# Hybrid decoder trunk: another order of the three products in the two-chunk steps of its linear attention

## The chip, the cores and the metric

The kernel runs on one core of a Trainium2 chip. The metric is the device time of one execution in microseconds (us), as the median of several runs. The core has five engines with a queue each: TensorE (PE, matrix products; its weight loads are listed apart as PEld), VectorE (DVE), ScalarE (ACT), GpSimd (POOL) and SyncE (SP, which issues DMAs). They meet through semaphores. PE writes into PSUM, which is divided into banks of 512 float32 columns on 128 partitions; DVE and ACT read the results from there.

## What is computed

The reference is one layer of a decoder trunk on 2048 tokens (and 16 meta tokens ahead of them) with 1024 channels. One input projection feeds two branches, a Mamba-2 scan (SSD) and gated linear attention (GLA); each goes through a gate and a projection, and an output projection with the residual and a final norm ends it. The change lies in the GLA branch:

```python
def gla_chunked(q, k, v, log_a, chunk, state0):
    ...
    def step(s, inp):
        qi, ki, vi, gi = inp
        o_inter = jnp.einsum('bhtk,bhkv->bhtv', qi * jnp.exp(gi), s)
        ...
        att = jnp.einsum('bhtk,bhsk,bhtsk->bhts', qi, ki, rel)
        o_intra = jnp.einsum('bhts,bhsv->bhtv', att, vi)
        g_last = gi[:, :, -1]
        k_dec = ki * jnp.exp(g_last[:, :, None, :] - gi)
        s_new = jnp.exp(g_last)[..., None] * s + jnp.einsum('bhsk,bhsv->bhkv', k_dec, vi)
        return s_new, o_inter + o_intra
```

There are 4 heads of 128 key and 256 value channels. Per chunk and head there are three products: the **state product** (queries times the state `s`), the **attention product** (attention matrix times values), and the **key product** (decayed keys times values). The first two are added and are the chunk's output. The third goes into the **state update**, which makes the state for the next chunk.

## The kernel before, in words

The tokens are cut into 4 blocks of 512 (`BLK`), each into 4 chunks of 128 (`NCH`). In the first part (up to about 1530 us) every block goes through 4 SSD groups and 4 GLA heads: `ssd_proj` and `gla_proj` are generators that do the projections on PE, and between their pieces `step()` advances the scans that are running beside them (`ssd_scan`, `gla_scan`, the gates, the loading of the next block). So a scan is a generator too, and what stands between two of its `yield`s goes into PE's queue in one piece, between two pieces of projection. The second part (gate, branch and output projections) isn't touched.

PE's and SP's queues hold their instructions in the order in which the code is written (`manual_schedule`). The framework orders those of DVE, ACT and POOL itself, by a model of the engines, and places the semaphores by what the tiles need.

`accum(ps, stat, mov, first, last)` (lines 189 to 191) is a product in three matmuls: both operands are split into a high and a low float32r part, and high x high, high x low and low x high are added in `ps`. The values (`got["v"]`), the decayed keys (`kdt`) and the attention matrix (`atp`) exist as such pairs; in the profile the values are named `tok`. The state product (line 846) is one float32 matmul, which appears twice in the trace (x2 per chunk).

The last stage of `gla_scan` goes through the chunks in a loop, lines 841 to 853, two chunks in each step, since it yields after every odd chunk. Per chunk there is one PSUM bank `po` from the pool `pc` (of two banks): columns 256 to 511 take the key product, columns 0 to 255 the sum of attention product and state product. PE does, for every chunk, the key product (line 844), the attention product (845) and the state product (846). DVE then does the state update (847), in place in `s_gla`, reading the key product in the bank. ACT copies the output half of the bank to `ot` (849) and sums its squares (851), after the update. The odd chunk's state product reads what the even chunk's update wrote. 4 blocks x 4 heads x 2 make 32 such steps with 64 chunks.

[...]

Of the kernel before, what the change touches and what calls it, by code (L numbers as in the profile page):

```python
# [14 lines left out]
P = 128  # L15
# [25 lines left out]
def trunk_kernel(ctx: ExitStack, tc: tile.TileContext, xm, xmt, w_feat, w_tok, w_zm, w_br, w_o,  # L41
                 cf32, cmsk, pvec, fnw, hvec, gw2, out):
    nc = tc.nc
# [5 lines left out]
    def mk(pool, shape, dt, tag, **kw):  # L49
        cnt[0] += 1  # L50
        return pool.tile(shape, dt, tag=tag, name=f"{tag}_{cnt[0]}", **kw)
# [83 lines left out]
    def bank(pool, tag):  # L135
        return mk(pool, [P, 512], F32, tag)
# [20 lines left out]
    s_gla = const.tile([P, GH, 256], F32, name="s_gla")  # L157
# [29 lines left out]
    def accum(ps, stat, mov, first, last, **kw):  # L187
        (sh, sl), (mh, ml) = stat, mov
        nc.tensor.matmul(ps, sh, mh, start=first, stop=False, **kw)  # L189
        nc.tensor.matmul(ps, sh, ml, start=False, stop=False, **kw)  # L190
        nc.tensor.matmul(ps, sl, mh, start=False, stop=last, **kw)  # L191
# [480 lines left out]
    def gla_proj(o, h):  # L672
        got = {"gs": []}
        keys = yield from gla_keys(o, h)
        last = o.b == nblk - 1
        if last and h == GH - 1:
            begin(gla_scan(o, h, *keys, got))
            yield
            got["v"] = yield from gla_values(o, h)
            yield  # L680
            yield from gla_gates(o, h - 1, held_gates.pop())
            yield from gla_gates(o, h, got["gs"])
        else:
            yield
            got["v"] = yield from gla_values(o, h)
            if last and h == GH - 2:
                begin(gla_scan(o, h, *keys, got))
                held_gates.append(got["gs"])
                yield
            else:  # L690
                yield
                yield from gla_gates(o, h, got["gs"])
                begin(gla_scan(o, h, *keys, got))
# [3 lines left out]
    def gla_scan(o, h, qs, kf, got):  # L697
# [19 lines left out]
        qg = mk(wk, [P, META + BLK], F32, "act", bufs=NACT)[:, :BLK]  # L717
# [57 lines left out]
        kdt = [mk(wk, [P, NCH, P], F32R, "kdt", bufs=2) for _ in range(2)]  # L775
# [54 lines left out]
        atp = [mk(wk, [P, NCH, P], F32R, "atp", bufs=2) for _ in range(2)]  # L830
# [10 lines left out]
        for c in range(NCH):  # L841
            po = bank(pc, "pc")
            vc = [t[:, c] for t in got["v"][0]]
            accum(po[:, 256:], [t[:, c] for t in kdt], vc, True, True)
            accum(po[:, :256], [t[:, c] for t in atp], vc, True, False)
            nc.tensor.matmul(po[:, :256], qg[:, c * P:(c + 1) * P], s_gla[:, h], start=False, stop=True)
            nc.vector.scalar_tensor_tensor(s_gla[:, h], s_gla[:, h], egl[:, c:c + 1], po[:, 256:],
                                           op0=ALU.mult, op1=ALU.add)
            nc.scalar.activation(ot[:, c], po[:, :256], AF.Copy)
            jk = mk(wk, [P, 256], BF16, "junk", bufs=1)  # L850
            nc.scalar.activation(jk, po[:, :256], AF.Square, accum_out=ssq[:, c:c + 1])
            if c % 2:
                yield
# [372 lines left out]
```

## Time and profile before

| | |
|---|---|
| median of 3 runs | 2328.28 us (2320.05 to 2328.89) |
| the profiled execution | 2335.47 us |
| its span, first to last instruction | 2333.7 us |
| mean granted clock of PE | 0.988 |
| PE busy | 2243.4 us |
| state products (L846) in the trace | 128 pieces, median 379 ns |
| state updates (L847) | 64, median 479 ns |

The profile is of one execution, by the hardware profiler. A row of its timeline has the start, the length, the engine, the line, the operation, what is written and read (by the program's names without numbers: `pc` is a bank of that pool) and the shapes; in brackets stands the idle time of the engine just before, and what ended it. Matmuls are pipelined, so one starts before the one ahead of it has ended, and their ends are modelled. A list of waits has per row who waited, for whom, how long in total and how often. In a list of the program's order `[waits DVE_49]` says that the instruction waits for a semaphore that DVE raises. No time is in such a list.

### The profile page before, as it was taken

What the parts mean: (1) busy time and instruction counts of PE and PEld (TensorE: products, weight loads), DVE (VectorE), ACT (ScalarE), POOL (GpSimd) and SP (SyncE); (2) the same over time, 40 slices, a digit from 0 to 9 for tenths busy, and PEclk for the clock granted to TensorE, in tenths of its full rate; (3) what the DMA queues carried; (4) which work ended last, traced back from release to release, by engine and by line L of the source; (5) the groups of instructions that cost most, each with busy time, mean ns of one, the idle gap of its engine ahead of it and who ended that gap; (6) DMA issues with size and microseconds to landing.
All of it is one profiled execution on the core that took longest, in us unless ns stands there. A gap on an engine that the chain in (4) does not pass through costs nothing.

```text
span 2333.7 us, 36472 instructions
## 1 busy us (share of the span) xinstructions
PE 2243.4 (96%) x12651; PEld 1956.5 (84%) x12651; DVE 1563.6 (67%) x2884; ACT 1188.9 (51%) x2764; POOL 687.6 (29%) x677
## 2 busy tenths in 40 slices
PE   6899999999999999999999999989999999999998
PEld 6889989888888988888988898868788888787886
DVE  5676766676675667566568655664679855788966
ACT  5665655465544455543456443464554454554443
POOL 3344433122321212221122200026424264423341
PEclk9999999999999999999999999999999999999999
DMA  7655865667786666777676655466668866778753
GB/s 254 225 203 200 293 234 195 210 206 222 264 271 190 207 221 211 253 244 234 187 236 214 216 168 164 140 222 207 221 227 275 283 224 215 260 247 276 226 189 108
DMA packets 300937, 515.89 MB, mean 221 GB/s; under 512 B 27616, under 2 KB 143584, under 8 KB 300752
## 3 DMA queue, kind: packets, MB, share of 16 engines
q1 hardware_dynamic: 221840, 422.15, 55.7%
q10 hardware_dynamic: 78912, 91.41, 11.3%
q8 instruction: 99, 1.62, 0.3%
q14 instruction: 86, 0.70, 0.1%
HBM read 366.26 MB, written 147.19 MB: 220 GB/s over the span
## 4 chain that ended last, share of the span: by engine, by line
PE 48%; DMA 9%; DVE 7%; issue 4%; ACT 3%; SPq 1%; POOL 1%; ACTq 0%; DVEq 0%; POOLq 0%
PE pj L189 7%; PE pj L191 7%; PE pj L190 7%; PE psa L189 4%; PE psa L191 4%; PE psa L190 4%; DMA br<-br_t 2%; PE psb L191 2%; PE psb L190 2%; PE psb L189 2%; PE pc L756 1%; DMA br<-gate_t 1%; DVE b L960 1%; DVE a L984 1%; DMA acc<-in_xmt 1%
## 5 line engine op out<-in xcount | busy, mean ns | idle before, releaser
L189 PE MATMUL pj<-u,whl 128*128 128x512 f32 (+1 forms) x1184 | 448.7, 379 | 13.4 <-ACT acc L503 8.5
L191 PE MATMUL pj<-u,whl 128*128 128x512 f32 (+1 forms) x1184 | 432.7, 365 | 0.8 <-POOL whl L177 0.8
L190 PE MATMUL pj<-u,whl 128*128 128x512 f32 (+1 forms) x1184 | 431.5, 364 | 0.0
L189 PE MATMUL pj<-whl,u 128*128 128x256 f32 (+1 forms) x992 | 289.1, 291 | 3.2 <-ACT u L252 2.2
L191 PE MATMUL pj<-whl,u 128*128 128x256 f32 (+1 forms) x992 | 282.3, 285 | 0.2 <-DVE u L257 0.2
L190 PE MATMUL pj<-whl,u 128*128 128x256 f32 (+1 forms) x992 | 282.1, 284 | 0.4 <-POOL whl L177 0.4
L189 PE MATMUL psa<-b,a 128*128 128x512 f32 x640 | 253.0, 395 | 21.0 <-ACT sn L1000 17.5
L189 PEld LDWEIGHTS pj<-u,whl 128*128 128x128 f32 x1184 | 226.7, 191 | 52.6 <-ACT acc L503 9.5
L191 PEld LDWEIGHTS pj<-u,whl 128*128 128x128 f32 x1184 | 225.8, 191 | 36.7 <-POOL whl L177 1.0
L190 PEld LDWEIGHTS pj<-u,whl 128*128 128x128 f32 x1184 | 226.8, 192 | 33.3
L190 PE MATMUL psa<-b,a 128*128 128x512 f32 x640 | 251.8, 393 | 0.0
L191 PE MATMUL psa<-b,a 128*128 128x512 f32 x640 | 251.5, 393 | 0.0
L984 DVE TENSOR_TENSOR a<-ar,a 128x512 fp32r<-128x512 f32 x160 | 153.0, 962 | 79.0 <-ACT a L983 78.6
L189 PEld LDWEIGHTS pj<-whl,u 128*128 128x128 f32 x992 | 190.0, 191 | 4.8 <-ACT u L252 2.3
L177 POOL TENSOR_TENSOR whl<-wr,whl 128x512 fp32r<-128x512 f32 (+1 forms) x100 | 134.6, 1354 | 196.2 <-ACT whl L176 147.5
L190 PEld LDWEIGHTS pj<-whl,u 128*128 128x128 f32 x992 | 189.9, 191 | 1.0 <-POOL whl L177 0.6
L191 PEld LDWEIGHTS pj<-whl,u 128*128 128x128 f32 x992 | 189.7, 191 | 0.8 <-DVE u L257 0.8
L80 POOL TENSOR_TENSOR wr<-wr 128x256 f32<-128x256 f32 x80 | 69.7, 871 | 383.6 <-DMA wr<-u 160.9
L960 DVE TENSOR_TENSOR b<-br,b 128x512 fp32r<-128x512 f32 x196 | 149.4, 784 | 45.0 <-ACT b L959 44.5
L974 POOL TENSOR_TENSOR as<-ar,ar 128x512 f32<-128x512 f32 x40 | 59.5, 1488 | 400.5 <-DMA ar<-in_w_br 100.5
L507 DVE SCALAR_TENSOR_TENSOR acc<-cin,hcw,acc 128x512 f32<-128x512 f32 (+1 forms) x192 | 159.6, 831 | 16.5 <-ACT acc L503 14.6
L959 ACT ACTIVATE b<-br 128x512 fp32r<-128x512 f32 x196 | 118.6, 626 | 94.6 <-DMA br<-br_t 34.2
(278 smaller groups left out, 5053.8 us busy)
## 6 DMA issues: line engine op xcount, KB each, us to landing
whl<-k_s SPq DMA_DIRECT2D x96, 512.0 KB, 4.2
whl<-k_g SPq DMA_DIRECT2D x96, 512.0 KB, 4.1
whl<-k_v SPq DMA_DIRECT2D x48, 512.0 KB, 4.1
whl<-k_z SPq DMA_DIRECT2D x36, 512.0 KB, 4.1
wr<-in_w_feat SPq DMA_DIRECT2D x64, 256.0 KB, 4.3
k_s<-whl SPq DMA_DIRECT2D x32, 512.0 KB, 3.7
cb<-cumd ACTq DMA_DIRECT2D x64, 256.0 KB, 5.7
y<-gg ACTq DMA_DIRECT2D x64, 256.0 KB, 4.7
```

What stands on the lines that cost most here:

```text
L80: nc.gpsimd.tensor_tensor(o, x, y, op=ALU.subtract)
L177: nc.gpsimd.tensor_tensor(hl[:, 1], raw, hl[:, 0].bitcast(F32), op=ALU.subtract)
L189: nc.tensor.matmul(ps, sh, mh, start=first, stop=False, **kw)
L190: nc.tensor.matmul(ps, sh, ml, start=False, stop=False, **kw)
L191: nc.tensor.matmul(ps, sl, mh, start=False, stop=last, **kw)
L507: nc.vector.scalar_tensor_tensor(acc, cin[:, k:k + tt], hcw[:, ti, k:k + 1], acc, op0=ALU.mult, op1=ALU.add)
L756: nc.tensor.matmul(ps[:, r * P:(r + 1) * P], kq[:, 2 * r * P:(2 * r + 1) * P], kq[:, (2 * r + 1) * P:(2 * r + 2) * P], start=True, stop=True)
L959: nc.scalar.activation(t[:, 0], raw, AF.Copy)
L960: nc.vector.tensor_tensor(t[:, 1], raw, t[:, 0].bitcast(F32), op=ALU.subtract)
L974: nc.gpsimd.tensor_tensor(s1, a21, a22, op=ALU.add)
L984: nc.vector.tensor_tensor(t[:, 1], src, t[:, 0].bitcast(F32), op=ALU.subtract)
```

## The change

The loop treats even and odd chunks differently. In an even chunk PE does the state product first, then the key product; the code of the state update comes next, and the attention product behind it. In an odd chunk it is key product, attention product, state product, as in every chunk before. Only the first matmul in a bank has `start=True`, where the attention product's first matmul had it as well before. The new lines are nine more, so line numbers behind the loop go up: the state update is L854, the state product L850 (odd) and L852 (even), ACT's copy L858.

```diff
         for c in range(NCH):
             po = bank(pc, "pc")
             vc = [t[:, c] for t in got["v"][0]]
-            accum(po[:, 256:], [t[:, c] for t in kdt], vc, True, True)
-            accum(po[:, :256], [t[:, c] for t in atp], vc, True, False)
-            nc.tensor.matmul(po[:, :256], qg[:, c * P:(c + 1) * P], s_gla[:, h], start=False, stop=True)
+            kv, av = ([t[:, c] for t in m] for m in (kdt, atp))
+            sg = dict(skip_group_check=True)
+            qs_ = po[:, :256], qg[:, c * P:(c + 1) * P], s_gla[:, h]
+            if c % 2:
+                accum(po[:, 256:], kv, vc, True, False, **sg)
+                accum(po[:, :256], av, vc, False, False, **sg)
+                nc.tensor.matmul(*qs_, start=False, stop=True, **sg)
+            else:
+                nc.tensor.matmul(*qs_, start=True, stop=False, **sg)
+                accum(po[:, 256:], kv, vc, False, False, **sg)
             nc.vector.scalar_tensor_tensor(s_gla[:, h], s_gla[:, h], egl[:, c:c + 1], po[:, 256:],
                                            op0=ALU.mult, op1=ALU.add)
+            if c % 2 == 0:
+                accum(po[:, :256], av, vc, False, True, **sg)
             nc.scalar.activation(ot[:, c], po[:, :256], AF.Copy)
```

## The prediction

> **What bounds the kernel now.** The page comes first, for the engine that is busiest.
>
> ```profile
> span 2333.7 us, 36472 instructions
> PE 2243.4 (96%) x12651; PEld 1956.5 (84%) x12651; DVE 1563.6 (67%) x2884; ACT 1188.9 (51%) x2764; POOL 687.6 (29%) x677
> ```
>
> TensorE (PE) is busy for 96% of the span, no other compute engine for more than 67%. The changed lines run between 326 and 1525 us, so I then asked for the busy time by stretches. The columns are the stretch and its length, the busy time of PE, its weight loads (PEld), DVE, ACT and POOL, the granted clock, and two figures on DMA.
>
> ```profile
> 327.00:330.70 3.70, 1.77 (x14) 1.51 (x12) 3.53 (x8) 2.07 (x7) 0.99 (x1) 1.00 0.85 286
> 330.80:334.10 3.30, 3.02 (x12) 2.84 (x13) 2.69 (x4) 3.30 (x12) 1.28 (x1) 0.50 0.16 50
> 706.30:709.50 3.20, 3.20 (x9) 2.45 (x8) 0.54 (x2) 1.05 (x5) 0.00 (x0) 0.50 0.00 0
> 1068.00:1075.00 7.00, 5.25 (x30) 4.45 (x29) 5.66 (x13) 4.89 (x16) 0.35 (x1) 1.00 0.55 191
> 300.00:1516.00 1216.00, 1195.14 (x7303) 1062.30 (x7304) 783.77 (x1721) 605.00 (x1565) 257.84 (x321) 0.99 0.66 213
> ```
>
> By the last row PE idles for 1216.00 - 1195.14 = 20.9 us in the 1216 us that hold nearly all attention steps. Time that PE newly waits there lengthens the run almost in full, and no more than those 20.9 us can be given back. The other rows are for the clock, below.
>
> Next the list of waits and the tile of the state, s_gla (us in total, times, and in the list the longest wait):
>
> ```profile
> PE pc L846 <- DVE s_gla L847: 7.5, 5, 2.7
> DVE s_gla L847 <- PE pc L846: 73.0, 40, 7.4
> L847 DVE SCALAR_TENSOR_TENSOR s_gla<-s_gla,egl,pc x64: 467/479/483, 330.6 to 1523.8; 128x256 f32<-128x256 f32 x64
> ```
>
> There are 64 state updates (L847), two in each of 32 steps. Of all these steps PE waited for the even chunk's update in only five, 7.5 us together. In 40 of 64 updates it was the reverse: DVE stood ready and waited for PE. So the update is mostly prompt, and today's order hides it. The timeline of one such step shows how (start, length, engine, line, [idle before]):
>
> ```profile
> 473.97 0.28 PE L189 MATMUL pc<-tok,kdt 128*128 128x256 f32 x1
> 474.08 0.28 PE L190 MATMUL pc<-tok,kdt 128*128 128x256 f32 x1
> 474.31 0.28 PE L189 MATMUL pc<-tok,atp 128*128 128x256 f32 x1
> 474.65 0.59 PE L846 MATMUL pc<-s_gla,act 128*128 128x256 f32 x2
> 474.89 0.47 PE L189 MATMUL pc<-tok,kdt 128*128 128x256 f32 x1
> 475.20 0.28 PE L190 MATMUL pc<-tok,kdt 128*128 128x256 f32 x1
> 475.28 0.48 DVE L847 SCALAR_TENSOR_TENSOR s_gla<-s_gla,egl,pc 128x256 f32<-128x256 f32 x1 [1.36 <-PE pc L846]
> 475.67 0.28 PE L191 MATMUL pc<-tok,atp 128*128 128x256 f32 x1
> 475.82 0.70 PE L846 MATMUL pc<-s_gla,act 128*128 128x256 f32 x2
> ```
>
> The even chunk's state product ends at 474.65 + 0.59 = 475.24, the update starts 0.04 later and ends at 475.76. Meanwhile PE goes through the odd chunk's key and attention products (six matmuls, one every 0.11 to 0.12 us) and starts the odd state product, which needs the update, at 475.82. Nothing is lost.
>
> **The change, part by part.** No matmul, DMA or copy is added or removed; the 14 matmuls of a step stand in another order. These are PE's rows of the first step before, from the last key matmul of the even chunk (bank pc_4080) to the odd chunk's state product (bank pc_4092); kdt are keys, atp the attention matrix, each as a high and a low part:
>
> ```order
> L191 MATMUL pc_4080<-tok_444_3057,kdt_3641 128x256
> L189 MATMUL pc_4080<-tok_444_3057,atp_3974 128x256 [waits Activation_49]
> L190 MATMUL pc_4080<-tok_445_3058,atp_3974 128x256
> L191 MATMUL pc_4080<-tok_444_3057,atp_3975 128x256 [waits DVE_49]
> L846 MATMUL pc_4080<-s_gla,act_3539 128x256
> L189 MATMUL pc_4092<-tok_444_3057,kdt_3640 128x256 [waits PE_49]
> L190 MATMUL pc_4092<-tok_445_3058,kdt_3640 128x256
> L191 MATMUL pc_4092<-tok_444_3057,kdt_3641 128x256
> L189 MATMUL pc_4092<-tok_444_3057,atp_3974 128x256 [waits Activation_49]
> L190 MATMUL pc_4092<-tok_445_3058,atp_3974 128x256
> L191 MATMUL pc_4092<-tok_444_3057,atp_3975 128x256 [waits DVE_49]
> L846 MATMUL pc_4092<-s_gla,act_3539 128x256 [waits DVE_49]
> ```
>
> And PE's rows of the even chunk now, from its state product (L852) on:
>
> ```order
> L852 MATMUL pc_4080<-s_gla,act_3539 128x256 [waits PE_49]
> L189 MATMUL pc_4080<-tok_444_3057,kdt_3640 128x256
> L190 MATMUL pc_4080<-tok_445_3058,kdt_3640 128x256
> L191 MATMUL pc_4080<-tok_444_3057,kdt_3641 128x256
> L189 MATMUL pc_4080<-tok_444_3057,atp_3974 128x256 [waits DVE_49,Activation_49]
> L190 MATMUL pc_4080<-tok_445_3058,atp_3974 128x256
> ```
>
> The end of the odd chunk now:
>
> ```order
> L191 MATMUL pc_4092<-tok_444_3057,kdt_3641 128x256
> L189 MATMUL pc_4092<-tok_444_3057,atp_3974 128x256 [waits Activation_49]
> L190 MATMUL pc_4092<-tok_445_3058,atp_3974 128x256
> L191 MATMUL pc_4092<-tok_444_3057,atp_3975 128x256
> L850 MATMUL pc_4092<-s_gla,act_3539 128x256
> ```
>
> Two things moved with the matmuls. The even attention product has a new wait for DVE at its first matmul, and the odd state product has lost its own. The odd state product reads what the even update wrote, so it can go without a wait only if PE has waited for that update already, and the sole DVE wait ahead of it is the new one. So PE now stands still between the even key product and the even attention product until the update is done. The two don't share a byte: the update reads columns 256 to 511 of the bank, the attention product writes columns 0 to 255, but the dependency is kept by the bank. Before, the update could run beside six matmuls; now beside none. Queued behind the waiting matmul are the nine matmuls up to the odd state product and the projections after it; ACT's copies of both chunks and DVE's odd update wait for those.
>
> [...]
>
> *The prompt step.* With the state product first at 0, the gaps of the rows above give the first key matmul at 0.24 (474.65 to 474.89), the second at 0.24 + 0.31 = 0.55 (474.89 to 475.20), the third at 0.67; it ends at 0.95. The update starts at 0.99 and ends at 1.47. How fast PE resumes is shown by a step in which it did wait, the first:
>
> ```profile
> 328.49 0.28 PE L191 MATMUL pc<-tok,atp 128*128 128x256 f32 x1
> 330.55 0.47 DVE L847 SCALAR_TENSOR_TENSOR s_gla<-s_gla,egl,pc 128x256 f32<-128x256 f32 x1
> 331.08 1.22 PE L846 MATMUL pc<-s_gla,act 128*128 128x256 f32 x2 [2.31 <-DVE s_gla L847]
> ```
>
> The update ends at 331.02 and PE starts at 331.08, 0.06 later. So the even attention product starts at 1.53 instead of 0.67 + 0.11 = 0.78, a stall of 0.75 us. The weights for it are not loaded ahead of the wait either. What that adds is seen in a short wait of today:
>
> ```profile
> 380.67 0.70 PE L846 MATMUL pc<-s_gla,act 128*128 128x256 f32 x2 [0.55 <-DVE s_gla L847]
> 381.02 0.47 PE L189 MATMUL pj<-u,whl 128*128 128x264 f32 x1
> 705.30 0.70 PE L846 MATMUL pc<-s_gla,act 128*128 128x256 f32 x2 [2.72 <-DVE s_gla L847]
> 1068.40 0.28 PE L189 MATMUL pc<-tok,kdt 128*128 128x256 f32 x1
> 1072.15 0.70 PE L846 MATMUL pc<-s_gla,act 128*128 128x256 f32 x2 [1.75 <-DVE s_gla L847]
> ```
>
> After it the next matmul comes 0.35 us later, against 0.24 in the prompt step: 0.1 more. Price of a prompt step: 0.85 us. Between 0.75 (loads hidden after all) and 0.85 I take the upper, since the wait stands on the load as well.
>
> *The late steps.* In five steps DVE comes late, and PE waits today by 2.31, 0.55, 2.72, 1.75 us and one smaller wait (7.5 in all). There the time at which PE resumes is set by DVE and stays. But nine matmuls (even attention, odd key and odd attention products), which ran ahead of that wait, now follow it: 9 x 0.117 = 1.05, with the load 1.15 us each. So today's 7.5 us of waits are not won back; they move ahead in the step.
>
> *In between* are steps in which DVE comes just in time today, but not for the earlier appointment:
>
> ```profile
> 482.55 0.28 PE L189 MATMUL pc<-tok,kdt 128*128 128x256 f32 x1
> 483.38 0.69 DVE L493 SCALAR_TENSOR_TENSOR tok<-tok,pj 128x512 f32<-128x512 f32 x1 [2.19 <-ACT tok L492]
> 483.98 0.48 DVE L847 SCALAR_TENSOR_TENSOR s_gla<-s_gla,egl,pc 128x256 f32<-128x256 f32 x1
> ```
>
> The step began at 482.55, so the update started at 1.43 and not at 0.99: 0.44 us more. Going through the 32 even updates in the timeline I find five like it, and three where DVE is about 0.13 late: 5 x 0.44 + 3 x 0.13 = 2.6 us.
>
> *The clock.* After the 2.31 and the 2.72 us of idling the granted clock is 0.50 for some 3.3 us (the rows of 330.80 and 706.30 above), after 1.75 us at 1072 it stays 1.00. The third late step will idle from the end of its even key product (1068.40 + 0.95 = 1069.35) to 1072.15, 2.8 us, longer than both that were halved: one more half-clock stretch, half of 3.3, 1.7 us. [...]
>
> *DVE, ACT, POOL, SP.* Where the first step's updates stand on DVE before:
>
> ```order
> L847 SCALAR_TENSOR_TENSOR s_gla<-s_gla,egl_3537,pc_4080 128x256 [waits PE_49]
> L714 TENSOR_TENSOR act_4104<-act_4104,act_3551 128x528 [waits Activation_49]
> L847 SCALAR_TENSOR_TENSOR s_gla<-s_gla,egl_3537,pc_4092 128x256 [waits PE_49]
> L719 TENSOR_TENSOR act_4116<-act_4116,act_3463 128x512 [waits Activation_49]
> L847 SCALAR_TENSOR_TENSOR s_gla<-s_gla,egl_3537,pc_4195 128x256 [waits PE_49]
> ```
>
> and now:
>
> ```order
> L854 SCALAR_TENSOR_TENSOR s_gla<-s_gla,egl_3537,pc_4080 128x256 [waits PE_49]
> L714 TENSOR_TENSOR act_4104<-act_4104,act_3551 128x528 [waits Activation_49]
> L719 TENSOR_TENSOR act_4116<-act_4116,act_3463 128x512 [waits Activation_49]
> L854 SCALAR_TENSOR_TENSOR s_gla<-s_gla,egl_3537,pc_4092 128x256 [waits DVE_49,PE_49]
> L854 SCALAR_TENSOR_TENSOR s_gla<-s_gla,egl_3537,pc_4195 128x256 [waits DVE_49,PE_49]
> ```
>
> The odd update went behind one instruction that isn't about it; all 32 even updates stand behind the same DVE work as before. The odd update has until the next step, 8.6 us on in the two steps shown (473.97 to 482.55), so its move costs nothing; if a later step's state product did come to wait, at most the 0.7 us of an L719. Some other DVE, ACT and POOL instructions change places with a neighbour; SP's queue is unchanged. These I put at 0, bounded by 2 us either way.
>
> *The sum.* 27 steps x 0.85 = 23.0; 5 x 1.15 = 5.8; 2.6 for the steps in between; clock 1.7: 33 us. Against it, PE waits for DVE and ACT elsewhere in the stretch for 20.9 - 7.5 = 13.4 us. A later PE may find some of those ready; but those engines mostly work on what PE gives them and are then later too. I take 4 off, between 0 and 13: +29 us. The profiled execution took 2335.5 us (its span 2333.7, 1.8 around it) and would take 2364.5; the median of the runs before is 7 us lower, 2328.3, which gives 2357.
>
> **The rivals.** *Not slower: the new wait is free.* The DVE wait in PE's row could be for the low part of the attention matrix alone, which DVE wrote long before, with the update still hidden. Then PE idles no longer than today: between no change and the 7.5 us of the five waits, 2321 to 2328. This decides if the even attention product starts within 0.2 us of the key product. For it: that low part does come from DVE. Against it: the odd state product's row has no DVE wait any more, and it must have the update. 4%.
>
> *Given back.* PE's other 13.4 us of waits vanish as PE arrives later: 33 - 13 = +20, 2348. For it: those waits are for DVE and ACT, which have idle time. Against: they sit in a few places, not behind each of 32 steps. 14%.
>
> *The clock falls further.* The three longest late steps idle for 2.8 to 3.8 us, and each could be halved for two stretches; with steps of 1.2 to 1.6 us joining in, four more stretches of 1.7 us: +36, 2364. Against it: 1.75 us of idling kept 1.00. 16%.
>
> *Every stall halves the clock.* 32 x 1.7 = 54 us more, 2411. The row of 1068 speaks against it. 1%.
>
> **How the numbers follow.** My forecast, +29, has 65%. Of the three runs before, the lowest lies 8 us below the median. The range goes from the given-back case less that (2340) to the clock case plus as much (2372), which takes in the 2 us of reordering. Within 0.5%, 11.6 us, is about what a measurement of this kernel can't tell from no change. Every case but the first lies beyond it, so slower has 0.95; the first is within it, 0.04, and 0.01 is left for faster.
>
> **What would show it.** Right: in the list of waits PE waits for s_gla's update about 32 times, 0.6 to 0.9 us each where DVE is prompt, on matmuls that read atp; no PE wait is left on the state product of L850; PE's busy time is about the same while its idle time in the attention stretch grows from 20.9 to about 50 us; ACT's copies and the odd update come some 0.8 us later in their step. Wrong: fewer than ten such waits, or the waits are there and the stretches between them are shorter than now, which is time given back; or a clock of 0.50 in many stretches.

## The result, and the profile after

| | before | changed |
|---|---|---|
| median of 4 runs each | 2325.50 us | 2356.45 us |
| lowest and highest | 2320.05, 2328.89 | 2353.54, 2358.64 |
| the profiled executions shown | 2335.47 us | 2358.64 us |

The ratio is 1.0126 (95% interval 1.0109 to 1.0142): slower, by 25 to 33 us. The page of the changed kernel has PE at the same work, within 2.3 us of 2243.4, in a longer span:

```profile
span 2356.8 us, 36562 instructions
PE 2245.7 (95%) x12651; PEld 1959.5 (83%) x12651; DVE 1566.9 (66%) x2884; ACT 1190.3 (51%) x2764; POOL 692.0 (29%) x677
```

So the time went into PE's waits. The list of PE's waits in the changed kernel, its first rows for the part with the attention steps (300 to 1550 us; total us, times, longest):

```profile
PE pc L189 <- DVE s_gla L854: 25.3, 30, 3.4
PE pc L189 <- ACT act L718: 6.3, 2, 3.2
PE pc L593 <- DVE sq L584: 3.6, 2, 2.5
```

30 + 2 = 32 waits on the first matmul of a product into a `pc` bank, one for each step, 31.6 us together. The five waits on the state product, 7.5 us before, are gone from the list. (The two put down to ACT are the steps at 703 and 1069 us. That matmul waits for several semaphores, and the list names the one that came last; in the timeline DVE's update ends 0.15 us ahead of it there as well.) The prompt step that the prediction looked at, now (here and below, rows between those shown are left out):

```profile
477.32 0.59 PE L852 MATMUL pc<-s_gla,act 128*128 128x256 f32 x2
477.57 0.47 PE L189 MATMUL pc<-tok,kdt 128*128 128x256 f32 x1
477.87 0.28 PE L190 MATMUL pc<-tok,kdt 128*128 128x256 f32 x1
477.99 0.28 PE L191 MATMUL pc<-tok,kdt 128*128 128x256 f32 x1
478.31 0.48 DVE L854 SCALAR_TENSOR_TENSOR s_gla<-s_gla,egl,pc 128x256 f32<-128x256 f32 x1 [1.02 <-PE pc L191]
478.93 0.36 PE L189 MATMUL pc<-tok,atp 128*128 128x256 f32 x1 [0.66 <-DVE s_gla L854]
479.13 0.28 PE L190 MATMUL pc<-tok,atp 128*128 128x256 f32 x1
480.03 0.59 PE L850 MATMUL pc<-s_gla,act 128*128 128x256 f32 x2
480.46 0.60 PE L449 MATMUL pt<-cst,alr 128*48 128x128 f32 x4
```

The key product's last matmul starts at 477.99 and lasts 0.28; the update begins at 478.31, 0.99 after the step's start, and lasts 0.48; only then does the even attention product start, 0.94 after the matmul ahead of it instead of 0.11 or 0.12. The odd state product at 480.03 follows without a wait. The whole step (to the next work on PE) takes 480.46 - 477.32 = 3.14 us. Before, it took 476.35 - 473.97 = 2.38, to this row:

```profile
476.35 0.60 PE L449 MATMUL pt<-cst,alr 128*48 128x128 f32 x4
```

### The profile page after: what moved, and what is told of

The parts are those of the page before. It is cut to its first block, busy times and chain, and to the rows that moved or that the text cites. A ratio compares the mean times of both kernels' runs of the same rounds, so it can differ in the third digit from the quotient of the medians.

```text
span 2356.8 us, 36562 instructions
## 1 busy us (share of the span) xinstructions
PE 2245.7 (95%) x12651; PEld 1959.5 (83%) x12651; DVE 1566.9 (66%) x2884; ACT 1190.3 (51%) x2764; POOL 692.0 (29%) x677
## 4 chain that ended last, share of the span: by engine, by line
PE 53%; DMA 7%; DVE 6%; issue 3%; ACT 3%; POOL 1%; SPq 0%; ACTq 0%; DVEq 0%; POOLq 0%
PE pj L189 7%; PE pj L191 7%; PE pj L190 7%; PE psa L189 5%; PE psa L190 5%; PE psa L191 5%; PE psb L190 2%; PE psb L191 2%; PE psb L189 2%; DMA br<-br_t 2%; DMA acc<-in_xmt 2%; PE psc L191 1%; PE psc L190 1%; PE psc L189 1%; PE pc L756 1%
## 5 line engine op out<-in xcount | busy, mean ns | idle before, releaser
L189 PE MATMUL psa<-b,a 128*128 128x512 f32 x640 | 256.0, 400 | 24.4 <-ACT sn L1009 20.8
L190 PE MATMUL psa<-b,a 128*128 128x512 f32 x640 | 254.5, 398 | 0.0
L191 PE MATMUL psa<-b,a 128*128 128x512 f32 x640 | 254.1, 397 | 0.0
```

## The experiments

The theory: the update reads the bank into which the even attention product writes, so that product waits for it, and PE stands still. The rivals: the other order as such, or what the scheduler moved, costs the time; or the clock does.

**The update's code behind the attention product.** State, key, attention product stay in the changed order; only the new wait goes.

```diff
             else:
                 nc.tensor.matmul(*qs_, start=True, stop=False, **sg)
                 accum(po[:, 256:], kv, vc, False, False, **sg)
+                accum(po[:, :256], av, vc, False, True, **sg)
             nc.vector.scalar_tensor_tensor(s_gla[:, h], s_gla[:, h], egl[:, c:c + 1], po[:, 256:],
                                            op0=ALU.mult, op1=ALU.add)
-            if c % 2 == 0:
-                accum(po[:, :256], av, vc, False, True, **sg)
```

> The changed order of matmuls, with the even chunk's state update written behind its attention product, so that the new wait is gone and nothing else. Theory (the cost is PE's stall between the even key product and the even attention product, made by the update that reads the same bank): the time of the kernel before, 2325 us, within 7 us, and PE waits for s_gla only in about five late steps, on the odd state product. Rival (the other order as such, the float32 state product ahead of the key product, or what the scheduler moved on DVE and ACT, costs the time): it stays at 2345 us or more.

Measured: 2329.99 us against 2327.05 for the kernel before on the same chip, ratio 1.0007 (0.9991 to 1.0023). The five late waits stand on the odd state product again, in the list of PE's waits:

```profile
PE pc L850 <- DVE s_gla L855: 7.8, 5, 2.7
```

By the interval the order of the matmuls costs between -2 and +5 us, of the 31 of the whole change; the place of the update among them makes the rest. The rival of the order falls.

**The even key product in a bank of its own.** The update stays where the changed kernel has it.

```diff
+            ko = po[:, 256:] if c % 2 else bank(pt, "pt")[:, :256]
...
-                accum(po[:, 256:], kv, vc, False, False, **sg)
-            nc.vector.scalar_tensor_tensor(s_gla[:, h], s_gla[:, h], egl[:, c:c + 1], po[:, 256:],
+                accum(ko, kv, vc, True, True, **sg)
+            nc.vector.scalar_tensor_tensor(s_gla[:, h], s_gla[:, h], egl[:, c:c + 1], ko,
```

> The changed kernel, with the even chunk's key product in a bank of its own (of the pool pt); the update is written at the same place as in the changed kernel. Theory (the dependency is kept by the bank): the wait at the even attention product goes, nine matmuls run beside the update instead of six, and the time is 2315 to 2328 us. Rival (the wait belongs to the place of the update in the code, whatever the bank): 2350 us or more, with about 30 waits of 0.6 us still on the attention product.

Measured: 2329.44 us, ratio 1.0006 (0.9990 to 1.0023); the upper end expected by the theory, 2328, is missed by 1.4 us, the rival by 20. The waits on the attention product are gone, and four late ones on the odd state product are left:

```profile
PE pc L851 <- DVE s_gla L855: 8.2, 4, 2.7
```

So the shared bank makes the wait. (The framework placed it. In this kernel a tile of `pc` is a whole bank, so the runs don't tell a rule by tile from one by bank, and none lets update and attention product run at once in one bank.) Nine matmuls beside the update win little over six: the prompt step takes 2.28 us here and 2.38 before, too little to show between the medians. The waits that are left belong to a late DVE, and more work on PE ahead of them does not shorten them in sum (8.2 us for four, 7.5 for five before).

**The wait kept, but covered.** The odd chunk's key and attention products, in the other bank, go ahead of the even attention product.

```diff
             if c % 2:
                 accum(po[:, 256:], kv, vc, True, False, **sg)
                 accum(po[:, :256], av, vc, False, False, **sg)
+                accum(pe_[:, :256], ae_, ve_, False, True, **sg)
                 nc.tensor.matmul(*qs_, start=False, stop=True, **sg)
             else:
                 nc.tensor.matmul(*qs_, start=True, stop=False, **sg)
                 accum(po[:, 256:], kv, vc, False, False, **sg)
+                pe_, ae_, ve_ = po, av, vc
             nc.vector.scalar_tensor_tensor(s_gla[:, h], s_gla[:, h], egl[:, c:c + 1], po[:, 256:],
                                            op0=ALU.mult, op1=ALU.add)
-            if c % 2 == 0:
-                accum(po[:, :256], av, vc, False, True, **sg)
-            nc.scalar.activation(ot[:, c], po[:, :256], AF.Copy)
...
+            for p_, c_ in ((pe_, c - 1), (po, c)) if c % 2 else ():
+                nc.scalar.activation(ot[:, c_], p_[:, :256], AF.Copy)
...
```

> The even attention product still stands behind the even update and waits for it, but the odd chunk's key and attention products (six matmuls, in the other bank) are put ahead of it. ACT's copies of the even chunk then come after the odd update's code. Theory (only the part of the update that nothing covers costs time): six matmuls last 0.7 us, the update 0.54 with its hand-over, so the prompt steps cost nothing and the time is 2320 to 2332 us. Rival (a wait at this place costs by itself, with the weight load that isn't loaded ahead, 0.3 us or more in each of 32 steps): 2335 to 2345 us.

Measured: 2342.11 us, ratio 1.0058 (1.0037 to 1.0078), 10 us above what the theory gave and within the rival's range. Yet the rival's reason is wrong. In the timeline, a prompt step and then one in which DVE is busy until just before:

```profile
472.26 0.59 PE L853 MATMUL pc<-s_gla,act 128*128 128x256 f32 x2
473.24 0.48 DVE L856 SCALAR_TENSOR_TENSOR s_gla<-s_gla,egl,pc 128x256 f32<-128x256 f32 x1 [1.03 <-PE pc L191]
473.63 0.28 PE L191 MATMUL pc<-tok,atp 128*128 128x256 f32 x1
473.78 0.39 PE L189 MATMUL pc<-tok,atp 128*128 128x256 f32 x1
474.67 0.60 PE L449 MATMUL pt<-cst,alr 128*48 128x128 f32 x4
...
482.82 0.39 PE L189 MATMUL pc<-tok,atp 128*128 128x256 f32 x1 [0.31 <-DVE s_gla L856]
484.29 0.94 PE L553 MATMUL pc<-act,act 128*128 128x128 f32 x6 [0.41 <-ACT junk L861]
```

The waiting matmul starts at 473.78, 0.15 after the one ahead, and the step takes 474.67 - 472.26 = 2.41 us against 2.38 before: a covered wait costs nothing in a prompt step. The time went elsewhere, as the list of PE's waits in this kernel shows:

```profile
PE pc L189 <- DVE s_gla L856: 9.4, 10, 2.5
PE pc L756 <- ACT junk L861: 4.7, 7, 1.0
PE pt L774 <- DVE act L714: 3.0, 2, 2.1
```

Ten steps wait for a DVE that is late, twice the five of before, since the wait now comes three matmuls earlier than the odd state product did. And ACT can copy the even chunk only behind the attention product, so both banks of `pc` come free later; PE's waits for ACT's squares (4.7 us; 1.3 in the trace of before) show it. Waits for the decayed keys (L714) went from 0.9 to 3.0 as well. These three make some 7 us of the 15 between the medians. This trace also has a wait of 2.2 us for a DMA into `whl` at the end of a step, and none of the traces of before has one of that length; whether the order brought it is open, and for the rest I have no cause that is shown.

**Odd chunks in the same order too.** 64 waits instead of 32.

```diff
-            if c % 2:
-                accum(po[:, 256:], kv, vc, True, False, **sg)
-                accum(po[:, :256], av, vc, False, False, **sg)
-                nc.tensor.matmul(*qs_, start=False, stop=True, **sg)
-            else:
-                nc.tensor.matmul(*qs_, start=True, stop=False, **sg)
-                accum(po[:, 256:], kv, vc, False, False, **sg)
+            nc.tensor.matmul(*qs_, start=True, stop=False, **sg)
+            accum(po[:, 256:], kv, vc, False, False, **sg)
...
-            if c % 2 == 0:
-                accum(po[:, :256], av, vc, False, True, **sg)
+            accum(po[:, :256], av, vc, False, True, **sg)
```

> Odd chunks too in the even chunk's order, so 64 instead of 32 places at which the attention product waits for the update of its own bank. Theory (each uncovered update costs 0.75 to 0.85 us of PE): 32 stalls more, about 24 to 30 us more than the changed kernel's 2356, so 2378 to 2388 us. Rival (half of the cost of the change is something else, such as the clock of the later stages): the second 32 stalls bring 15 us or less, 2371 us or below.

Measured: 2393.94 us, ratio 1.0281 (1.0254 to 1.0307): 37 us above the changed kernel, 6 more than the theory's upper end, far from the rival's 15. (The changed kernel was not run again beside it; the kernel before was, and its median lay 1.6 us above that of the first comparison.) From PE's list for the whole run, and the second wait of a prompt step in the timeline:

```profile
PE pc L189 <- DVE s_gla L849: 52.5, 62, 3.5
PE pc L189 <- ACT act L718: 6.7, 2, 3.9
...
488.30 0.48 DVE L849 SCALAR_TENSOR_TENSOR s_gla<-s_gla,egl,pc 128x256 f32<-128x256 f32 x1 [1.55 <-PE pc L191]
488.93 0.36 PE L189 MATMUL pc<-tok,atp 128*128 128x256 f32 x1 [0.66 <-DVE s_gla L849]
```

62 + 2 are the 64 waits, one for each chunk. A prompt odd wait has the 0.66 us of an even one. The second 32 came out dearer: 31 steps took 146.4 us, 37.5 more than in the changed kernel's first trace. Six of the odd updates stand behind other work in DVE's queue that ends late, and PE idles for 1.35 to 2.03 us there. Besides, PE's clock was at half for 41 us between 300 us and the last step, against 10 to 17 in the three traces of the changed kernel. How the excess divides between the two I have not worked out.

**Second and third traces of both kernels.** One trace each had left two things that the theory doesn't give: less time between the steps, more after them.

> The changed kernel once more, for a second trace. In the first trace the later part (from the first gate product on) took 809 us with 41 us at half clock, against 799 and 21 in the trace of the kernel before; no instruction stands in another order there. If that is chance, this trace has 794 to 803 us there and again 25 us more in the steps. If it belongs to the change, it has 806 us or more there again.

> The kernel before once more, for a second trace, beside the second one of the changed kernel. If the given-back time between the steps (1110.8 us before, 1100.1 in the changed kernel) is real, this trace has about 1111 us between the steps; if the trace of before merely had a bad draw of half-clock stretches and DVE waits there, it has 1100 to 1105.

> The changed kernel a third time. The 31 steps take 109 us within 2 in every trace if the stalls are what the theory says, since they come from the program's order; the later part and the stretches between the steps may vary by 10 us. The rival, that the clock makes part of the cost, wants traces of the changed kernel to differ in the steps too.

> The kernel before a third time: 83.5 us within 2 for the 31 steps by the theory; between the steps and in the later part whatever chance gives, which says how far single traces can be compared there.

From the timelines I added up the lengths of 31 steps (from a step's first matmul to the next work on PE), the stretches between them, and the time from the first gate product to the end, in us. The 32nd step is left out: behind it PE waits for ACT in any case (4.84 us before, 3.49 in the changed kernel), and its length fell from 7.52 to 6.86.

```
                      profiled execution   31 steps   between   later part
before                2335.5                83.5      1110.8     799.1
before, 2nd           2322.8                82.4      1105.1     796.3
before, 3rd           2322.1                82.9      1105.5     795.5
update behind         2323.8                83.9      1103.8     796.0
changed               2358.6               108.9      1100.1     809.2
changed, 2nd          2354.3               110.8      1103.3     801.9
changed, 3rd          2349.7               110.3      1099.9     799.5
key in its own bank   2338.2                80.2      1109.1     805.9
wait covered          2342.1                90.0      1113.4     800.0
odd chunks too        2398.9               146.4      1112.1     801.3
```

The second and third trace of the changed kernel list 30 + 2 waits on the attention product again. In both kernels the steps repeat within 2 us: 82.9 on average before, 110.0 in the changed kernel, 27.1 more. Between them the changed kernel is 6.0 faster (1107.1 to 1101.1), so time is given back, though the first pair of traces showed too much of it, and the second trace of before, at 1105.1, lies on the edge of what was expected of a bad first draw. The later part, in which no instruction of DVE or ACT has changed places, took 6.5 us more on average; without the first trace of the changed kernel (809.2, with 41 us at half clock against 17 to 25 in the other five) it would be 3.7, and 799.5 and 799.1 lie side by side. The 801.9 of the second trace is in the range expected of chance, and the kernel with the key product in its own bank, whose prompt steps have no stall, has 805.9 (31 us at half clock): a long later part doesn't need the stall. Whether any of it belongs to the change, and what makes it, is open.

## Why the prediction was right

*The mechanism* was as predicted: 32 waits at the even attention product, none left on the state product. The two experiments that removed the wait, in different ways, gave back all of the time, within 5 us.

*The prompt step* was priced at 0.75 for the stall and 0.1 for weights that aren't loaded ahead. Measured: 3.14 - 2.38 = 0.76. The update's start came out exactly (0.99). The load is there (it starts at 478.90, 0.11 behind the update's end; the attention product starts at 1.61, not 1.53, and the next matmul 0.20 later), but it moved rather than came: the odd state product of before waited for its update and its weights too (the update ended at 475.76, the load started at 475.81), and the next work came 0.53 behind it, now 0.43. So a cost that the step of before already had was counted as new, 27 x 0.1 = 2.7 us too much. And the last of the 32 steps, priced like the others, cost nothing, since PE waits for ACT behind it.

*The late steps*, priced at 1.15, cost 1.84, 1.07, 0.46, 1.75 and 0.76 in the first pair of traces, 5.9 together against 5.8. That is partly luck: the second and third traces give 9.3 and 8.2, with half clock inside some of these steps. Today's waits did move ahead and weren't won back.

*The steps in between* were priced at 0.85 + 0.44. The one quoted went from 2.75 to 3.56, 0.8 more: before, its odd state product already came a little late (0.26 us behind the attention product instead of 0.15), and this lateness I counted again. About 2 us too much. So the steps cost 27 us, where the sum had 31.

*The clock*: one more half-clock stretch was predicted for the step at 1069, and the trace has it (0.50 from 1074.30, behind 3.14 us of idling), but the rule behind it, that idling of 2.3 us or more halves the clock, failed. At 703 PE idled for 3.20 us and the clock stayed at 1.00; before, 2.72 us at this step had halved it, and in the third trace of the changed kernel 3.18 us did (rows at 703, at 1069, and of the third trace):

```profile
707.14 0.36 PE L189 MATMUL pc<-tok,atp 128*128 128x256 f32 x1 [3.20 <-ACT act L718]
1073.31 0.36 PE L189 MATMUL pc<-tok,atp 128*128 128x256 f32 x1 [3.14 <-ACT act L718]
709.37 0.55 PE L189 MATMUL pc<-tok,atp 128*128 128x256 f32 x1 [3.18 <-ACT act L718]
```

Stretches of the changed kernel (three: one with the 3.20 us, one behind it, one behind the 3.14 us) and of its third trace (one, from 0.65 us before the end of the 3.18 us on), with the columns as before:

```profile
703.00:708.50 5.50, 2.30 (x17) 2.04 (x16) 5.17 (x13) 4.26 (x14) 0.00 (x0) 1.00 0.60 199
709.04:712.45 3.41, 3.41 (x17) 2.82 (x16) 0.35 (x1) 0.75 (x3) 0.00 (x0) 1.00 0.00 0
1074.30:1077.60 3.30, 3.30 (x11) 2.64 (x10) 0.54 (x2) 1.14 (x6) 0.00 (x0) 0.50 0.02 9
708.72:712.13 3.41, 2.76 (x12) 2.70 (x12) 1.71 (x4) 1.99 (x7) 0.00 (x0) 0.50 0.19 77
```

So the length of the idling alone did not decide: 3.20 us left the clock at 1.00, where 3.14 us in the same trace, 3.18 us in the third and 2.72 us before were followed by 0.50. What did decide is not shown.

The size of the term held all the same: between 300 us and the last step the traces of before have 9.1 us at half clock on average (13.7, 6.8, 6.8), those of the changed kernel 12.5 (10.2, 17.1, 10.2), one stretch more. The step at 703 cost only 0.46 us because DVE's update ended 4.00 us into the step instead of 4.66; the clock shows in the stretch behind it, which was 1.6 us shorter than before.

*Given back*: 4 us taken, 6.0 measured. PE's idle time in the stretch, predicted to rise to about 50 us, rose to 1228.60 - 1191.34 = 37.3, partly for this and partly since the trace counts as idle only what is left after a matmul's modelled end (0.66 of a stall of 0.82):

```profile
300.00:1528.60 1228.60, 1191.34 (x7298) 1060.54 (x7297) 780.65 (x1720) 606.18 (x1564) 259.93 (x320) 1.00 0.65 211
```

*The total* of 2357 against 2356.45 is thus better than its parts, and in that lucky: the steps were 4 us too dear, what was given back 2 too small, and the 6.5 us of the later part weren't foreseen at all. (In the three pairs of traces 27.1 - 6.0 + 6.5 makes 27.6 us; the medians differ by 31, with an interval from 25 to 33.) The median of before, measured again, also came out 2.8 us lower, so the change cost 31 us against 29 predicted. Of the rivals, the free wait is refuted by the 32 waits, and the clock at every stall by one half-clock stretch more instead of 32; the other two were questions of amount. Shorter stretches between the steps were named as a sign of being wrong; they are 6.0 us shorter, of which 4 were in the sum.

## What to carry to other kernels

When an engine has to read half of a PSUM bank while PE could fill the other half, look where the reader stands in the program: in these runs what PE was to write into that bank after it waited for it, whatever the columns (32 waits in 32 steps, 64 with the odd chunks in the same order). Give the two halves different banks (ratio 1.0006 here), or put work of another bank between (1.0058), and count that a wait moved ahead meets the reader earlier in its own queue (ten late steps here instead of five). A wait that vanishes from one instruction's row in the program's order has to be looked for in an earlier row; it was that row that told this result.

## What the runs showed of the hardware beyond that

The length of PE's idling by itself did not tell whether its clock would be halved: in the first trace of the changed kernel 3.14 us were followed by 0.50 and 3.20 us by 1.00, in its third 3.18 us at the step of those 3.20 by 0.50, and in the first trace of before 2.31 and 2.72 us by 0.50 and 1.75 us by 1.00. What else it takes, no run here shows. And single traces of one kernel differ by up to 10 us outside the code in question (799.5 to 809.2 in the later part), while the steps themselves repeat within 2: a difference of half a per cent between two traces has to be located, not only summed.
